# A two-layer attention and ConvFFN trunk on one core: the residual's split copy 288 bytes further on, two small reorderings beside it

## The chip, the core and the metric

One core of one Trainium2 chip runs the whole program in one launch. The metric is the device time of one execution in microseconds (us). Before the change three runs gave 598.50, 600.23 and 598.19 us: median 598.5 us.

## What is computed

A causal decoder trunk of two layers over 256 tokens of width 1024, in float32, with a final RMSNorm. Layer 0 mixes MoBA and differential attention, layer 1 dilated attention and a latent (MLA) attention; each layer ends in a gated ConvFFN with 2816 channels.

```python
def rmsnorm(x, g):
    y = xf * lax.rsqrt(jnp.mean(xf * xf, axis=-1, keepdims=True) + EPS)
    return y * g
...
h = h + even_mixer(rmsnorm(h, even_norm1[i]), ...)       # layer 0
h = h + odd_mixer(rmsnorm(h, odd_norm1[i]), ...)         # layer 1
h = h + conv_ffn(rmsnorm(h, ffn_norm[layer]), ...)       # after each mixer
...
return rmsnorm(h, final_norm)
# in odd_mixer, the latent part
q  = heads(rmsnorm(cq,  q_norm)  @ w_uq, ...)
kv = heads(rmsnorm(ckv, kv_norm) @ w_ukv, ...)
# in conv_ffn
u, g = jnp.split(h @ w_in, 2, axis=-1)
return (gelu(causal_conv(g)) * u) @ w_out
```

## The kernel before

**Splitting.** TensorE multiplies in the type fp32r. To keep float32 accuracy every operand is split into a rounded high part and a remainder, and a product a*b is made as three matmuls: high*high, low*high, high*low. Weights come in 100 pieces of up to 1 MB from HBM (`raw`, queue of SP), ScalarE makes the high part `whi` (line 152), VectorE the low part `wlo` (line 148). They are read once, so the program streams about 105 MB of weights and keeps TensorE busy beside it.

**The residual.** `hT` holds the residual, 1024 channels as 8 blocks `k` of 128 partitions, 256 tokens wide. `xs` (line 232) holds its split copy, scaled by the norm's gain: for each `k` 256 high values and behind them 256 low values, so one `k` is 2,048 bytes of a partition and `xs` is 16,384. `make_xhat` writes it (line 240 on ScalarE the high half, line 242 on VectorE the low half): once at the start and once in each of three `close_phase` calls. All input projections of both mixers and both FFNs read it.

**Who reads `xs`, and as which operand.** A TensorE matmul has a stationary operand (loaded first, the rows PEld LDWEIGHTS) and a moving one that streams past it.

- `passmajor` and `colmajor` (lines 296 to 311): weight stationary, 256 columns of `xs` moving, three matmuls for each `k` and weight block. The program has 1,152 such matmuls.
- `product` (line 903) in the FFN blocks f = 5 to 21 of each layer: for each `k` one matmul of the high weight with high and low halves together (512 columns of `xs`), and one of the low weight with the high half (256 columns). That is 17 x 2 x 8 = 272 pairs in a layer, 544 in all.
- `vjob` (line 313): `xs` is stationary here, 512 columns of weights move; 3 calls of `v_units` x 2 x 8 x 3 = 144 matmuls.

The other large group are the output projections: `proj_tile` (line 482), with weights stationary and 256 columns of an activation tile `o` moving, and in the last FFN `proj_tail` (line 850), with `o` stationary and 512 or 256 columns of weights moving. In layer 1 `uq_unit` and `ukv_unit` (lines 722 and 737) move 256 columns of the latent tiles `cqh`, `cql`, `ckr`.

**Where the tiles lie.** Pools are laid out one behind another in each partition. The built program places `hT` at byte 129,312 and `xs` at byte 137,504, which is 32 past a multiple of 64 and 288 past a multiple of 512. All `whi` and `wlo` buffers are also 288 past a multiple of 512. All tiles of pool `two` (`o`, `cqh`, `cql`, `ckr`, `qk` and others) are 64 past one. Pools `tmp`, `work` and `two` lie behind `xs`.

**Order.** TensorE's order is written by hand for the whole program. In the start and in the FFN main loop the other engines' order is by hand too; in the attention stages a scheduler orders ScalarE, VectorE and GpSimd. The norm's scale is not applied to `xs` but later: squares of the residual are summed by four small matmuls (`pss`), `rsqrt` (line 256) makes the scale, and its broadcast (`psb`) multiplies what the projections leave.

**The latent stage (`u0`, line 665).** After the projections `cq` and `ckv` are in the banks `pc` and `pk`, ScalarE and VectorE split them into `cqh`, `cql`, `ckr` (lines 675 and 676); then ScalarE squares both (678, 679) and GpSimd adds the two halves of the first square (680). `col_sums` in `u2` sums the squares by matmuls (`pss<-ones,sqc`).

**The last norm (lines 953 to 977).** For each of five tiles of the result `TAIL`, ScalarE squares with an accumulated sum (959), VectorE multiplies the tile by the gain into `y` (960). With the last tile of a row block VectorE makes the mean (966), GpSimd the power -0.5 (969), ScalarE and VectorE scale one half of `y` each (973, 975), and two DMAs write them.

Of the kernel before, what the change touches and what calls it, by code (L numbers as in the profile page):

```python
# [22 lines left out]
F32R = mybir.dt.float32r  # L23
AF = mybir.ActivationFunctionType
ALU = mybir.AluOpType
# [3 lines left out]
S = 256  # L29
D = 1024  # L30
KD = D // 128
# [72 lines left out]
def trunk(ctx, tc, x, rel_bias, small, lam_p, wpack, fin_g, onehot, addrow, tab, out):  # L104
    nc = tc.nc
# [3 lines left out]
    xpool = ctx.enter_context(tc.tile_pool(name="xpool", bufs=1))  # L109
# [10 lines left out]
    def t2(name, dt=F32, shape=(128, 2, S)):  # L120
        return two.tile(list(shape), dt, name=name, tag="t2")
# [4 lines left out]
    def pair(a):  # L126
        return a.rearrange("p (a b) -> p a b", a=2)
# [101 lines left out]
    subg = consts.tile([128, 1], F32)  # L229


    xs = xpool.tile([128, KD, 2, S], F32R, name="xs")
    xh, xl = xs[:, :, 0], xs[:, :, 1]
    sqs = {}

# [319 lines left out]
    def two_pairs(ca, cb):  # L555
        a, b = need(ca), need(cb)
        pa, pb = bank("pd"), bank("pd")
        colmajor([(pa[:, 0:S], True, a, 0), (pa[:, S:], False, a, 128),
                  (pb[:, 0:S], True, b, 0), (pb[:, S:], False, b, 128)])
        return pa, pb  # L560

    def stats1(env):
        env['r_col'] = norm_cols()
        env['r_diag'] = diags(env['r_col'], 2)
# [95 lines left out]
    def odd_layer():  # L660
# [4 lines left out]
        def u0():  # L665
            pc, pk = box['p'] = two_pairs('ocq', 'ock')
            stats1(env)
            cqh, cql = t2("cqh", F32R), t2("cql", F32R)
            ckr = t2("ckr", F32R)
            s1, s2 = t2("sqc"), t2("sqk", shape=(128, S))  # L670
            for i in range(3):
                src = pc[:, i * S:(i + 1) * S] if i < 2 else pk[:, 0:S]
                hi, lo = (cqh[:, i], cql[:, i]) if i < 2 else (ckr[:, 0], ckr[:, 1])
                g = gcol[:, QNORM + i:QNORM + i + 1]
                nc.scalar.activation(hi, src, AF.Copy, scale=g)
                nc.vector.scalar_tensor_tensor(lo, src, g, hi.bitcast(F32), op0=ALU.mult,
                                               op1=ALU.subtract)
            nc.scalar.activation(s1, pair(pc), AF.Square)
            nc.scalar.activation(s2, pk[:, 0:S], AF.Square)
            nc.gpsimd.tensor_tensor(s1[:, 0], s1[:, 0], s1[:, 1], op=ALU.add)  # L680
            kt = t2("krt")
            nc.vector.tensor_tensor(kt[:, 0], pk[:, S:], tab_t, op=ALU.mult)
            box.update(cqh=cqh, cql=cql, ckh=ckr[:, 0], ckl=ckr[:, 1], sq=[[s1[:, 0]], [s2]], kt=kt)
# [79 lines left out]
        def u6():  # L763
            ukv_unit(1)
            uq_unit(2)
            uq_unit(3)

        units = [(None, u0), (None, u1), (None, u2), kc0[0], (None, u3), (None, u5), (None, u6)]
        units += qk_units(env, 'oq1', ('q2', 'q3'), 'r_q') + qk_units(env, 'ok1', ('k2', 'k3'), 'r_bc')
        units += v_units(env, 'ovc', 'vc')  # L770
# [13 lines left out]
    def ffn(l, final):  # L784
# [65 lines left out]
        def proj_tail(f, i):  # L850
            w = weights(f)
            (oh, ol), (hi, lo) = acts[f], w
            tb, c0, c1 = TAIL[i]
            a = box['acc'][i][:, :c1 - c0]
            s = slice(tb * 128, (tb + 1) * 128)
            mm(a, oh[:, s], hi[:, f % 2, c0:c1], False, False)
            mm(a, ol[:, s], hi[:, f % 2, c0:c1], False, False)
            mm(a, oh[:, s], lo[:, f % 2, c0:c1], False, f == NF - 1)

        if final:  # L860
            fin_t = [t2("fin", shape=(128, 512)) for _ in range(2)]
# [88 lines left out]
        def piece(t, tb, c0, c1):  # L950
            return t[2 * tb + c0 // 512][:, c0 % 512:c0 % 512 + c1 - c0]

        for i, (tb, c0, c1) in enumerate(TAIL):
            for f in range(NF - LAGF, NF):
                proj_tail(f, i)
            h, o = box['acc'][i][:, :c1 - c0], piece(y, tb, c0, c1)
            q = i if tb == 0 else i - 2
            t = t2("fsq", shape=(128, c1 - c0))
            nc.scalar.activation(t, h, AF.Square, accum_out=ss[tb][:, q:q + 1])
            nc.vector.tensor_tensor(o, h, fin_t[c0 // 512][:, c0 % 512:c0 % 512 + c1 - c0], op=ALU.mult)  # L960
            if q == 0:
                nc.vector.tensor_scalar(ss[tb][:, 0:1], ss[tb][:, 0:1], EPS * D, None, op0=ALU.add)
            if tb == 1 and q == 1:
                nc.vector.tensor_add(ss[tb][:, 0:1], ss[tb][:, 0:1], ss[tb][:, 1:2])
            if c1 == D:
                nc.vector.tensor_scalar(ss[tb][:, q:q + 1], ss[tb][:, q:q + 1], ss[tb][:, 0:1], 1.0 / D,
                                        op0=ALU.add, op1=ALU.mult)
                r = ss[tb][:, 3:4]
                nc.gpsimd.tensor_tensor(r, ss[tb][:, q:q + 1], mhalf[:, 0:1], op=ALU.pow)
                for c in range(2):  # L970
                    o = y[2 * tb + c]
                    if c == 0:
                        nc.scalar.activation(o, o, AF.Copy, scale=r)
                    else:
                        nc.vector.tensor_scalar(o, o, r, None, op0=ALU.mult)
                    (nc.scalar if c == 0 else nc.sync).dma_start(
                        out[tb * 128:(tb + 1) * 128, c * 512:(c + 1) * 512], o)
# [32 lines left out]
    def late_loads():  # L1010
# [6 lines left out]
        return lam_t  # L1017
    even_layer()
    ffn(0, False)
    odd_layer()  # L1020
    ffn(1, True)


# [68 lines left out]
```

## Time and profile before

| | |
|---|---|
| runs before, us | 598.50, 600.23, 598.19 (median 598.5) |
| profiled execution, us | 597.86, of which the span from first to last instruction is 596.1 |
| granted TensorE clock, mean over the span | 0.998 of full speed (2.4 GHz) |
| TensorE matmul busy | 588.3 us, 99% of the span |
| VectorE, ScalarE, GpSimd busy | 74%, 58%, 12% |
| HBM read | 104.92 MB, 178 GB/s over the span |

The profiled execution lies 0.64 us, or 0.1%, under the median. Matmuls overlap in the records (one's duration reaches past the start of the next), so TensorE's pace is read from the starts of successive matmuls, not from durations: the start of a later row less the start of an earlier one, divided by the matmuls between them. A row `x2` stands for two matmuls.

### The profile page before, as it was taken

Reading aid. Unit: us, or ns where it says so; the run is one execution under the profiler, and the core shown is the slowest. Engines: PE = TensorE matmul, PEld = TensorE weight load, DVE = VectorE, ACT = ScalarE, POOL = GpSimd, SP = SyncE. Lnnn points to the kernel's source line nnn. Section 1 sums busy time; section 2 is a strip of 40 time slices with the busy share of each in tenths; the row PEclk is TensorE's granted clock in tenths of the full one; section 3 lists DMA queues with packets and bytes.
Section 4 is the critical chain, followed back from the end, with each engine's and each line's share of the span. In section 5 each row is a group of like instructions: output and inputs, shape, how many; then the busy total and the mean of one; then the engine's idle time right before and its main releaser. Section 6 shows DMA issues by size and latency. Waiting matters only on the chain.

```text
span 596.1 us, 10372 instructions
## 1 busy us (share of the span) xinstructions
PE 588.3 (99%) x4078; PEld 542.7 (91%) x4078; DVE 441.1 (74%) x789; ACT 348.3 (58%) x643; POOL 69.7 (12%) x81
## 2 busy tenths in 40 slices
PE   9999999999999999999999999999999999999996
PEld 9989989999999999999999998999988888888885
DVE  5795966779777777877696975558967778777752
ACT  6757656548566555665554755646665556655532
POOL 1000001032011011101034000005110111001110
PEclk9999999999999999999999999999999999999999
DMA  8966645425544655455425343344535554554301
GB/s 293 383 230 222 222 142 191 164 82 205 211 163 189 213 212 192 165 208 194 165 103 221 134 145 137 142 172 147 213 142 211 212 196 167 203 196 167 132 1 71
DMA packets 20265, 106.67 MB, mean 179 GB/s; under 512 B 2478, under 2 KB 6008, under 8 KB 8568
## 3 DMA queue, kind: packets, MB, share of 16 engines
q1 hardware_dynamic: 16424, 101.68, 46.7%
q10 hardware_dynamic: 3632, 3.80, 2.1%
q8 instruction: 32, 0.52, 0.3%
q0 software_dynamic: 160, 0.52, 0.3%
q14 instruction: 17, 0.14, 0.1%
HBM read 104.92 MB, written 1.08 MB: 178 GB/s over the span
## 4 chain that ended last, share of the span: by engine, by line
PE 94%; issue 2%; POOL 2%; ACT 1%; DVE 1%; POOLq 0%; ACTq 0%
PE pd L124 52%; PE acc L124 26%; PE pv L124 6%; PE pS L124 2%; PE pO L124 2%; PE puq L124 1%; PE warm L124 1%; POOL sqt L251 1%; PE pukv L124 1%; PE pT L374 0%; PE pT L375 0%; PE pT L376 0%; PE psb L124 0%; PE pss L124 0%; POOL sqc L680 0%
## 5 line engine op out<-in xcount | busy, mean ns | idle before, releaser
L124 PE MATMUL pd<-xs,whi 128*128 128x256 f32 (+1 forms) x1312 | 326.3, 330 | 0.0
L124 PE MATMUL pd<-xs,wlo 128*128 128x256 f32 x928 | 252.2, 281 | 0.0
L148 DVE TENSOR_TENSOR wlo<-raw,whi 128x1024 fp32r<-128x1024 f32 (+1 forms) x191 | 233.8, 1249 | 20.3 <-ACT whi L152 20.2
L124 PEld LDWEIGHTS pd<-xs,whi 128*128 128x128 f32 x1312 | 218.2, 190 | 22.9 <-ACT sqt L247 0.6
L152 ACT ACTIVATE whi<-raw 128x1024 fp32r<-128x1024 f32 (+1 forms) x191 | 193.6, 1040 | 59.2 <-PE pd L124 20.5
L124 PEld LDWEIGHTS pd<-xs,wlo 128*128 128x128 f32 x928 | 172.4, 190 | 0.0
L124 PE MATMUL acc<-o,whi 128*128 128x256 f32 x608 | 108.7, 281 | 0.0
L124 PEld LDWEIGHTS acc<-o,whi 128*128 128x128 f32 x608 | 92.7, 188 | 1.0 <-issue 0.2
L124 PE MATMUL acc<-o,wlo 128*128 128x256 f32 x304 | 84.7, 279 | 0.0
L911 ACT ACTIVATE lowp<-pd 128x256 f32<-128x256 f32 x68 | 25.8, 379 | 79.8 <-PE pd L124 79.8
L807 POOL TENSOR_TENSOR ge<-ge,gbuf 128x256 f32<-128x256 f32 x44 | 37.1, 845 | 291.1 <-ACT ge L806 291.1
L912 DVE TENSOR_TENSOR ug<-pd,lowp 128x256 f32<-128x256 f32 x68 | 28.5, 420 | 50.3 <-ACT lowp L911 50.3
L124 PE MATMUL acc<-whi,o 128*128 128x512 f32 (+1 forms) x220 | 58.2, 350 | 0.2 <-ACT o L812 0.2
L124 PEld LDWEIGHTS acc<-o,wlo 128*128 128x128 f32 x304 | 57.1, 188 | 0.0
L124 PEld LDWEIGHTS acc<-whi,o 128*128 128x128 f32 x220 | 38.3, 188 | 7.5 <-ACT o L812 0.7
L124 PE MATMUL acc<-wlo,o 128*128 128x512 f32 (+1 forms) x110 | 38.6, 351 | 0.0
L813 DVE TENSOR_TENSOR o<-ge,o 128x256 fp32r<-128x256 f32 x44 | 19.0, 438 | 21.5 <-ACT o L812 21.5
L363 ACT ACTIVATE ex<-sc,nm 128x256 f32<-128x256 f32 (+1 forms) x56 | 24.8, 444 | 15.4 <-DVE nm L360 12.0
L794 ACT ACTIVATE t<-gbuf,ccol 128x256 f32<-128x256 f32 x44 | 26.4, 601 | 12.0 <-DVE gbuf L935 10.1
L812 ACT ACTIVATE o<-ge 128x256 fp32r<-128x256 f32 x44 | 18.4, 418 | 23.1 <-POOL ge L807 23.1
L124 PE MATMUL pv<-whi,xs 128*128 128x512 f32 x96 | 30.1, 395 | 0.0
L242 DVE SCALAR_TENSOR_TENSOR xs<-hT,gcol,xs 128x256 fp32r<-128x256 f32 x32 | 24.3, 803 | 5.3 <-ACT xs L240 5.3
(153 smaller groups left out, 501.2 us busy)
## 6 DMA issues: line engine op xcount, KB each, us to landing
raw<-in_wpack_dram SPq DMA_DIRECT2D x91, 1024.0 KB, 4.8
raw<-in_wpack_dram SPq DMA_DIRECT2D x5, 512.0 KB, 6.0
Tt<-btab ACTq DMA_DIRECT2D x3, 512.0 KB, 5.8
raw<-in_wpack_dram SPq DMA_DIRECT2D x4, 256.0 KB, 5.0
raw_t<-in_wpack_dram SPq DMA_DIRECT2D x4, 256.0 KB, 5.7
Tt<-btab ACTq DMA_DIRECT2D x1, 1024.0 KB, 6.3
hT<-in_x_dram ACTq DMA_DIRECT2D x4, 128.0 KB, 4.1
hT<-in_x_dram SPq DMA_DIRECT2D x2, 256.0 KB, 5.5
```

Of the source, the lines that this page charges most:

```text
L124: nc.tensor.matmul(o, l, r, start=start, stop=stop, skip_group_check=True)
L148: nc.vector.tensor_tensor(lo[:, s], raw, hi[:, s].bitcast(F32), op=ALU.subtract)
L152: nc.scalar.activation(splits[i][:, s], raw, AF.Copy)
L242: nc.vector.scalar_tensor_tensor(xl[:, k], hT[:, k], gcol[:, g0 + k:g0 + k + 1], xh[:, k].bitcast(F32), op0=ALU.mult, op1=ALU.subtract)
L251: eng.tensor_tensor(sqs['a'], sqs['a'], t, op=ALU.add)
L363: nc.scalar.activation(e[:, a:b], t[:, a:b], AF.Exp, bias=nm[:, i:i + 1], scale=-1.0, accum_out=den[:, i:i + 1])
L794: nc.scalar.activation(t1, g[:, 2:], AF.Identity, bias=col(f, 3), scale=col(f, 2))
L807: nc.gpsimd.tensor_tensor(ge, ge, gbuf[f % 3][:, 0, 2:], op=ALU.mult)
L812: nc.scalar.activation(o[:, 0], ge, AF.Copy)
L813: nc.vector.tensor_tensor(o[:, 1], ge, o[:, 0].bitcast(F32), op=ALU.subtract)
L911: nc.scalar.activation(lowp, p[:, S:], AF.Copy)
L912: nc.vector.tensor_tensor(t[:, i], p[:, :S], lowp, op=ALU.add)
```

## The change

Three edits.

1. The tile for `xs` is made 128 elements (512 bytes) longer, and `xs` starts 72 elements (288 bytes) into it. In the built program the residual's copy then starts at byte 137,792, which is a multiple of 64 and 64 past a multiple of 512, as the tiles of pool `two` are. The pools behind it move by 512 bytes, so their places within 512 bytes are what they were; `hT`, `whi` and `wlo` stay where they were.
2. In `u0` the three instructions on squares stand ahead of the split.
3. In the last norm, for a row block's last tile, the product with the gain stands behind the mean.

```diff
-    xs = xpool.tile([128, KD, 2, S], F32R, name="xs")
+    xbuf = xpool.tile([128, KD * 2 * S + 128], F32R, name="xs")
+    xs = xbuf[:, 72:72 + KD * 2 * S].rearrange("p (k a s) -> p k a s", k=KD, a=2)
     xh, xl = xs[:, :, 0], xs[:, :, 1]
...
             s1, s2 = t2("sqc"), t2("sqk", shape=(128, S))
+            nc.scalar.activation(s1, pair(pc), AF.Square)
+            nc.gpsimd.tensor_tensor(s1[:, 0], s1[:, 0], s1[:, 1], op=ALU.add)
+            nc.scalar.activation(s2, pk[:, 0:S], AF.Square)
             for i in range(3):
...
-            nc.scalar.activation(s1, pair(pc), AF.Square)
-            nc.scalar.activation(s2, pk[:, 0:S], AF.Square)
-            nc.gpsimd.tensor_tensor(s1[:, 0], s1[:, 0], s1[:, 1], op=ALU.add)
             kt = t2("krt")
...
-            nc.vector.tensor_tensor(o, h, fin_t[c0 // 512][:, c0 % 512:c0 % 512 + c1 - c0], op=ALU.mult)
+            if c1 < D:
+                nc.vector.tensor_tensor(o, h, fin_t[c0 // 512][:, c0 % 512:c0 % 512 + c1 - c0], op=ALU.mult)
...
             if c1 == D:
                 nc.vector.tensor_scalar(ss[tb][:, q:q + 1], ss[tb][:, q:q + 1], ss[tb][:, 0:1], 1.0 / D,
                                         op0=ALU.add, op1=ALU.mult)
+                nc.vector.tensor_tensor(o, h, fin_t[c0 // 512][:, c0 % 512:c0 % 512 + c1 - c0], op=ALU.mult)
                 r = ss[tb][:, 3:4]
```

No engine gains or loses an instruction, and TensorE's order is the same to the last matmul. Two pieces move.

ScalarE in `u0`, before (`sqc` and `sqk` are the squares, `cqh` and `ckr` the high parts of the split, `whi` weight pieces):

```order
L152 ACTIVATE whi<-raw 128x1024 x3
L675 ACTIVATE cqh<-pd,gcol 128x256
L152 ACTIVATE whi<-raw 128x1024 x2
L675 ACTIVATE cqh<-pd,gcol 128x256
L675 ACTIVATE ckr<-pd,gcol 128x256
L678 ACTIVATE sqc<-pd 128x512
L679 ACTIVATE sqk<-pd 128x256
L152 ACTIVATE whi<-raw 128x1024 x4
```

and now:

```order
L152 ACTIVATE whi<-raw 128x1024 x3
L672 ACTIVATE sqc<-pd 128x512
L674 ACTIVATE sqk<-pd 128x256
L679 ACTIVATE cqh<-pd,gcol 128x256
L152 ACTIVATE whi<-raw 128x1024
L679 ACTIVATE ckr<-pd,gcol 128x256
L679 ACTIVATE cqh<-pd,gcol 128x256
L152 ACTIVATE whi<-raw 128x1024 x5
```

Both squares have moved ahead of three split instructions and two weight pieces, and one weight piece has moved behind the split.

VectorE at the end of the program, the second row block, before (`fss` holds the sums of squares, `y` the result):

```order
L960 TENSOR_TENSOR y<-acc,fin 128x256
L964 TENSOR_TENSOR fss_6522<-fss_6522 128x1
L960 TENSOR_TENSOR y<-acc,fin 128x256
L966 TENSOR_SCALAR fss_6522<-fss_6522 128x1
L975 TENSOR_SCALAR y<-y,fss_6522 128x512
```

and now:

```order
L962 TENSOR_TENSOR y<-acc,fin 128x256
L966 TENSOR_TENSOR fss_6522<-fss_6522 128x1
L968 TENSOR_SCALAR fss_6522<-fss_6522 128x1
L970 TENSOR_TENSOR y<-acc,fin 128x256
L978 TENSOR_SCALAR y<-y,fss_6522 128x512
```

The mean (966, now 968) has moved ahead of one product with the gain. In the first row block the same two instructions have changed places.

## Rows read from the trace of the kernel before

**Rows 1.** The page, part 1: engine, busy us, share of the span, instructions

```profile
PE 588.3 (99%) x4078; PEld 542.7 (91%) x4078; DVE 441.1 (74%) x789; ACT 348.3 (58%) x643; POOL 69.7 (12%) x81
```

**Rows 2.** Waits, TensorE: who waited for whom, us in total, times, longest

```profile
PE pss L124 <- POOL sqc L680: 0.6, 1, 0.6
PE acc L124 <- ACT o L812: 0.2, 1, 0.2
```

**Rows 3.** Timeline, TensorE, layer 1 input projections: start us, us, engine, line, operation

```profile
303.92 0.40 PE L124 MATMUL pd<-xs,whi 128*128 128x256 f32 x2
...
314.00 0.40 PE L124 MATMUL pd<-xs,whi 128*128 128x256 f32 x2
```

**Rows 4.** Timeline, TensorE, output projection of layer 1's mixer, end

```profile
388.02 0.40 PE L124 MATMUL acc<-o,whi 128*128 128x256 f32 x2
...
401.67 0.40 PE L124 MATMUL pd<-xs,whi 128*128 128x256 f32 x2
```

**Rows 5.** Timeline, TensorE, end of layer 0's FFN, 120 matmuls of its output projection

```profile
288.71 0.40 PE L124 MATMUL acc<-o,whi 128*128 128x256 f32 x2
...
302.85 0.40 PE L124 MATMUL pd<-xs,whi 128*128 128x256 f32 x2
```

**Rows 6.** Timeline, TensorE, latent projections of layer 1

```profile
330.11 0.28 PE L124 MATMUL puq<-cqh,whi 128*128 128x256 f32 x1
...
331.16 0.40 PE L124 MATMUL pukv<-ckr,whi 128*128 128x256 f32 x2
```

**Rows 7.** Timeline, TensorE, products of FFN blocks 5 and 7 of layer 0

```profile
148.99 0.40 PE L124 MATMUL pd<-xs,whi 128*128 128x512 f32 x1
...
154.64 0.41 PE L124 MATMUL acc<-o,whi 128*128 128x256 f32 x2
...
165.84 0.39 PE L124 MATMUL pd<-xs,whi 128*128 128x512 f32 x1
...
171.39 0.40 PE L124 MATMUL acc<-o,whi 128*128 128x256 f32 x2
```

**Rows 8.** Timeline, TensorE, weights moving: vjob of layer 0, then proj_tail of layer 1

```profile
85.05 0.62 PE L124 MATMUL pv<-whi,xs 128*128 128x512 f32 x2
...
89.82 0.40 PE L124 MATMUL acc<-o,whi 128*128 128x256 f32 x2
...
441.41 0.62 PE L124 MATMUL acc<-whi,o 128*128 128x512 f32 x2
...
443.50 0.40 PE L124 MATMUL acc<-whi,o 128*128 128x256 f32 x2
```

**Rows 9.** Groups by shape, TensorE: xcount, then busy us and mean ns of one

```profile
L124 PE MATMUL pd<-xs,wlo 128*128 128x256 f32 x928 | 252.2, 281 | 0.0
L124 PE MATMUL pd<-xs,whi 128*128 128x512 f32 x544 | 190.5, 392 | 0.0
L124 PE MATMUL pd<-xs,whi 128*128 128x256 f32 x768 | 135.9, 287 | 0.0
```

**Rows 10.** Timeline, ScalarE and GpSimd, stage u0 of layer 1

```profile
314.73 0.46 ACT L675 ACTIVATE cqh<-pd,gcol 128x256 fp32r<-128x256 f32 x1
...
319.18 0.60 ACT L678 ACTIVATE sqc<-pd 128x512 f32<-128x512 f32 x1 [0.69 <-DVE cql L676]
...
315.13 1.63 POOL L259 TENSOR_TENSOR r_col<-rs,mhalf 128x2 f32<-128x2 f32 x1 [5.59 <-DVE rs L258]
319.85 1.80 POOL L680 TENSOR_TENSOR sqc<-sqc 128x256 f32<-128x256 f32 x1 [3.09 <-ACT sqc L678]
```

**Rows 11.** Timeline, all engines, the end of the program

```profile
590.75 0.42 DVE L960 TENSOR_TENSOR y<-acc,fin 128x256 f32<-128x256 f32 x1 [0.92 <-ACT fsq L959]
591.09 0.21 DVE L966 TENSOR_SCALAR fss<-fss 128x1 f32<-128x1 f32 x1
591.37 0.56 POOL L969 TENSOR_TENSOR fss<-fss,mhalf 128x1 f32<-128x1 f32 x1 [4.61 <-DVE fss L966]
```

**Rows 12.** Windows: stretch, its length, then busy us (and instructions) of PE, PEld, DVE, ACT, POOL

```profile
401.00:436.00 35.00, 35.00 (x286) 34.55 (x285) 31.51 (x44) 23.69 (x38) 11.53 (x11) 1.00 0.50 183
```

## The prediction

> **What bounds the kernel now.** I read the share of each engine first, then who waited for whom, then the starts of matmuls in the timeline. TensorE is busy 588.3 of the 596.1 us of the span [rows 1], and its waits for other engines are tenths of a us: 0.6 us once for the latent squares, 0.2 us once for an activation [rows 2]. So the kernel is a single stream of some four thousand matmuls, and its time is the pace of that stream. A wait can give back less than 1 us; a change of pace counts for every matmul. What is to be seen next is that the pace is not the same everywhere, although the engine is granted its full 2.4 GHz, where 256 columns take 106.7 ns.
>
> - With 256 columns of `xs` moving, 84 matmuls stand between starts 303.92 and 314.00 [rows 3]: 10.08 us / 84 = 120.0 ns each, 13.3 ns over the columns.
> - With 256 columns of `o` moving past the same kind of weights, 117 matmuls stand between 388.02 and 401.67 [rows 4]: 13.65 / 117 = 116.7 ns, 10.0 ns over the columns. At the end of layer 0's FFN it is 14.14 us for 120 [rows 5]: 117.8 ns.
> - With the latent tiles moving, 9 matmuls stand between 330.11 and 331.16 [rows 6]: 116.7 ns.
>
> The operations, the type, the weights' buffers and the run of three matmuls into one place are the same. What sets `xs` apart is where it lies: 32 bytes past a multiple of 64, while `o`, `cqh`, `cql` and `ckr` lie on one. The latent rows matter because they are made like an input projection and still go at the faster pace.
>
> **Edit 1, the place of `xs`, is the large term.** After it `xs` starts on a multiple of 64, and indeed at the same place within 512 bytes as `o`, against weights that stay where they are. So where `xs` moves, the nearest row is that of `o`.
>
> *256-column matmuls.* All matmuls into `pd` that move 256 columns are 928 + 768 [rows 9]; 544 of the 928 belong to products, which leaves 1,152. The gain of one lies between 0 (the place doesn't matter) and 120.0 - 116.7 = 3.3 ns; by rows 5 it is 2.2 ns. The sum is 2.5 to 3.8 us by the two paces; I take 3.2 us. Not all of it stays: between layer 1's norm and the first output projection TensorE already waits 0.2 us for an activation [rows 2], and VectorE is busy 31.51 of 35 us there [rows 12]. The norm's chain does not get shorter, so of the 0.8 us that the 240 matmuls there could gain I let 0.5 us turn into more of that wait, and keep 2.7 us.
>
> *Products.* FFN block 7 has 16 pairs between 165.84 and 171.39 [rows 7]: 5.55 / 16 = 346.9 ns for 768 columns, which take 320.0; so 13.4 ns over for each of two matmuls, the same excess as the 256-column ones with `xs` have. No row of this kernel has 512 columns of an aligned tile moving past weights. Bounds: nothing, or the pace of rows 4 for both (10.0 ns over, 340.0 a pair, 6.9 less), and by rows 5 (11.2 over) 342.4, 4.5 less. For 544 pairs [rows 9] that is 0, 2.5 or 3.8 us; I take 5.7 ns, so 3.1 us, because the equal excess says that one cause is at work in both shapes. As a cover for a faster FFN, VectorE has the rest of its time: it is busy 74% over the span [rows 1], and a block that is 1.5% shorter asks for 1% more of it.
>
> *`vjob`.* Here `xs` is stationary and weights move: 21 matmuls between 85.05 and 89.82 [rows 8], 227.1 ns each. In the last FFN weights move too, but past `o`, an aligned stationary: 9 matmuls between 441.41 and 443.50 [rows 8], 232.2 ns. After the change `xs` is aligned as `o` is, so I take the slower pace: 144 x 5.1 ns = 0.7 us lost. Bounds: 0 and 1 us.
>
> What is written to `xs`, and the pools behind it (moved by 512 bytes), I cost at nothing: VectorE and ScalarE are not waited for where that happens beyond what stands above, and the pools keep their place within 512 bytes.
>
> **Edit 2, the squares.** The sum on GpSimd ran from 319.85 for 1.80 us [rows 10], because ScalarE squared only at 319.18 after waiting for VectorE, and TensorE waited for its end: 0.6 us of idle matmul time [rows 2], 0.7 with the weight load that starts afresh. ScalarE was at the first part of the split at 314.73 [rows 10]; now the square stands there and ends at about 315.4. GpSimd is in its power until 315.13 + 1.63 = 316.76 [rows 10] and can end the sum by 318.6 even at its slow 1.80 us, some 2.5 us ahead of need. The wait goes wholly: -0.7 us. The split of the latents moves back by the two squares (some 1 us), and a weight piece behind it by about as much. `cqh` is first read at 330 [rows 6], so the cover is more than 10 us; without it 1 us would be lost. What is late next is nothing: the matmuls behind `pss` have their operands.
>
> **Edit 3, the last scale.** The end of the program is a chain of waits: product with the gain 590.75, mean 591.09, power 591.37, scaling, DMA [rows 11]. The mean takes the product's place and starts 591.09 - 590.75 = 0.34 us earlier; the product then runs under the power (0.42 against 0.56 us) and is done before the scaling on VectorE. -0.3 us, between 0.1 and 0.4.
>
> **The sum.** -2.7 - 3.1 + 0.7 - 0.7 - 0.3 = -6.1 us against the profiled execution's 597.86, which gives 591.8. That execution lies 0.64 us under the median of the three runs; I forecast 592.0 us.
>
> **A rule that speaks against edit 1.** The rows give 120.0 and 116.7 ns for the same shape in two places [rows 3, 4]. The Trainium skill (TensorE: Matmul & The Clock Gate, Step-by-step: what each phase is for) gives TensorE two independent read ports, so that loading weights takes nothing from the running matmul, and (SBUF — State Buffer, Specifications) lines of 16 bytes, on which `xs` started before as it does now. By these pages edit 1 changes no pace, and the time would be that of the first rival. Rows 3, 4 and 6 disagree: neither rule accounts for the 3.3 ns.
>
> **The rivals.**
>
> 1. *The place of `xs` changes nothing.* The difference between 120.0 and 116.7 ns would come from the order in which banks are filled, or from what ran ahead. For it: `acc` and `pd` use banks in another way, and `o` itself goes at 116.7 and 117.8 [rows 4, 5]. Against it: the latent rows, built like `pd`, go at 116.7 [rows 6]. Only edits 2 and 3 count: 597.86 - 1.0 = 596.9 us.
> 2. *Products keep their pace.* The pair may be held by the load of the second weight under a long matmul, not by the moving operand. Then -2.7 + 0.7 - 1.0 = -3.0: 594.9 us. Against it stands only the equal excess of 13.4 ns.
> 3. *Products fall into their slow pace, and the others keep theirs.* Block 5 of the same FFN took 148.99 to 154.64 for the same 16 pairs [rows 7]: 353.1 ns a pair, 6.2 more than block 7. The same matmuls can settle at another pace, then, and operands placed differently settle slower in rows 8. If all pairs went so: 544 x 6.2 ns = +3.4 us, with +0.7 for `vjob` and -1.0 that is +3.1: 601.0 us. It decides only if the 256-column matmuls gain less than about 1 us; with their 2.7 the two cancel and the time is within 1 us of before. Against it: past weights placed as here, an aligned moving tile is never slower than `xs` in any row.
>
> **How the numbers follow.** A measurement of this kernel can tell about 0.3%, 1.8 us, from no change. The forecast (both shapes gain, at paces between rows 4 and 5 or a little beyond) has 0.66, with its own range 589.0 to 594; rival 2 has 0.15; rival 1 has 0.12; rival 3 has 0.07. Forecast and rival 2 are faster by more than 1.8 us; rival 1 lies on the edge (1.6 us under the median), of which I count a third as faster. Faster 0.85, same 0.08, slower 0.07. The range goes from 588.8 (3.8 + 3.8 + 0.7 + 0.3 gained, nothing lost, and 0.5 more if the 528 output matmuls of layer 0's FFN go from the pace of rows 5 to that of rows 4) to 597.4, which takes in rivals 1 and 2 with the spread of the runs, and leaves out rival 3 and the edges of the forecast.
>
> **What would show it.** In the profile after: the same stretch of `pd<-xs` with 256 columns starts every 117 to 118 ns, not 120.0 (edit 1 right); products stand at 340 to 343 ns a pair, not 347; `pv` goes at about 232 ns. TensorE has no wait for `sqc`, and its square runs at 315. The power at the end starts 0.2 us after the mean with the product beside it. If the pair stands at 347, rival 2 holds; if `pd` stands at 120.0, rival 1; a pair at 353 is rival 3. The forecast is wrong as a whole if the pace does not follow the place of the moving tile.

## The result and the profile after

| | before | after |
|---|---|---|
| median of 6 runs each, us (lowest to highest) | 598.50 (597.77 to 600.23) | 594.62 (594.06 to 595.54) |
| profiled execution, us; its span | 597.86; 596.1 | 594.06; 592.3 |
| granted TensorE clock over the span | 0.998 | 1.0 |
| TensorE matmul busy, us | 588.3 | 584.7 |

The ratio is 0.9934, with a 95% interval of 0.9922 to 0.9945: 3.9 us faster. The forecast was 592.0 us, 2.6 us lower, with the range 588.8 to 597.4. The clock does not explain the gain: of the six executions after, one had a granted clock of 0.997 and took 594.09 us, another 1.0 and took 594.06. One execution further down stands apart and is left out of its kernel's median and ratio: of ten of the kernel with triples at 32 bytes one took 3304.54 us, the other nine 595.95 to 598.37.

TensorE is still the whole bound. The page's part 1 of the changed kernel (engine, busy us, share, instructions) answers to [rows 1]:

```profile
PE 584.7 (99%) x4078; PEld 538.9 (91%) x4078; DVE 441.5 (75%) x789; ACT 347.8 (59%) x643; POOL 69.7 (12%) x81
```

Its waits (who for whom, us in total, times, longest) answer to [rows 2]. The wait for `sqc` is gone and the one for `o` is as long as it was; the wait for `xs` is at the program's start, before the first projection. Both kernels also wait once for 1.0 us at the very start, in the matmuls of `warm`.

```profile
PE pd L124 <- ACT xs L241: 0.5, 1, 0.5
PE acc L124 <- ACT o L813: 0.2, 1, 0.2
```

The timeline of TensorE (start us, us, engine, line, operation), end of layer 0's FFN and the first projections of layer 1, for [rows 5] and [rows 3]:

```profile
287.31 0.40 PE L124 MATMUL acc<-o,whi 128*128 128x256 f32 x2
...
301.31 0.40 PE L124 MATMUL pd<-xs,whi 128*128 128x256 f32 x2
...
312.51 0.50 PE L124 MATMUL pss<-ones,sqt 128*128 128x1 f32 x4
```

From 301.31 to 312.51 stand 96 matmuls with 256 columns of `xs`: 11.20 / 96 = 116.7 ns, where it was 120.0. The 120 of `o` ahead of them take 14.00 us, 116.7 ns each, where they took 117.8, although nothing about `o` was changed.

The same view at FFN block 5 and at `vjob` of layer 0, for [rows 7] and [rows 8]:

```profile
148.22 0.39 PE L124 MATMUL pd<-xs,whi 128*128 128x512 f32 x1
...
153.77 0.40 PE L124 MATMUL acc<-o,whi 128*128 128x256 f32 x2
```

```profile
84.75 0.40 PE L124 MATMUL pv<-wlo,xs 128*128 128x512 f32 x1
...
89.89 0.28 PE L124 MATMUL acc<-o,whi 128*128 128x256 f32 x1
```

Sixteen pairs in 5.55 us are 346.9 ns a pair. Block 5 was at 353.1 and has come down to this; block 7 was here already, and stayed. `vjob` has 22 matmuls in 5.14 us: 233.6 ns, where it was 227.1.

Stage `u0` on four engines, for [rows 10], and the program's end, for [rows 11]:

```profile
312.91 0.58 ACT L672 ACTIVATE sqc<-pd 128x512 f32<-128x512 f32 x1
...
313.29 1.63 POOL L260 TENSOR_TENSOR r_col<-rs,mhalf 128x2 f32<-128x2 f32 x1 [5.25 <-DVE rs L259]
314.89 0.74 POOL L673 TENSOR_TENSOR sqc<-sqc 128x256 f32<-128x256 f32 x1
314.95 0.97 DVE L275 TENSOR_TENSOR diag<-ident,r_col 128x256 f32<-128x256 f32 x1 [0.60 <-POOL r_col L260]
...
315.65 0.28 PE L124 MATMUL pd<-xs,wlo 128*128 128x256 f32 x1
316.07 0.67 PE L124 MATMUL psb<-diag,ones 128*128 128x256 f32 x2
```

```profile
587.23 0.21 DVE L968 TENSOR_SCALAR fss<-fss 128x1 f32<-128x1 f32 x1 [0.92 <-ACT fsq L960]
587.36 0.41 DVE L970 TENSOR_TENSOR y<-acc,fin 128x256 f32<-128x256 f32 x1
587.52 0.55 POOL L972 TENSOR_TENSOR fss<-fss,mhalf 128x1 f32<-128x1 f32 x1 [4.86 <-DVE fss L968]
```

GpSimd adds the squares right behind its power, at 314.89 in place of 319.85, and takes 0.74 us in place of 1.80. But VectorE's `diag`, which starts 0.06 us behind it, takes 0.97 us here and 0.42 in the other three places of the program (and here before), and TensorE's `psb` waits for it: from 315.65 to 316.07 is 0.30 us more than one matmul's pace. At the end the product runs beside the power. In the kernel before, VectorE started a weight piece together with GpSimd's sum of [rows 10]:

```profile
319.85 1.22 DVE L148 TENSOR_TENSOR wlo<-raw,whi 128x1024 fp32r<-128x1024 f32 x1
```

The tally, from the starts of all 4,078 matmuls of the two traces, grouped by shape and operand:

| what | forecast, us | measured, us | how |
|---|---|---|---|
| 256 columns of `xs`, 1,152 | -2.7 | -3.4 | 119.8 to 116.8 ns each |
| products, 544 pairs | -3.1 | -0.3 | 347.4 to 346.8 ns a pair |
| `vjob`, 144 | +0.7 | +0.8 | 227.7 to 233.4 ns |
| squares | -0.7 | -0.5 | the wait gone, a shorter one for `diag` come |
| last scale | -0.3 | -0.3 | from the last matmul's start to the span's end: 6.15 to 5.88 us |
| 256 columns of `o`, 912 | 0 | -0.7 | 117.4 to 116.7 ns |
| `proj_tail`, 330 | 0 | -0.1 | |
| waits and starts elsewhere, most of them before 63 us | 0 | +0.7 | the rest |
| span | -6.1 | -3.8 | 596.1 to 592.3 |

The time up to 63 us, where most of the last row but one lies, differs by 0.2 to 0.3 us either way between this profile and those of two kernels below that have the same paces there (`xs` at 32 bytes, the sum on VectorE). The one large term that failed is products.

### The profile page after: what moved, and what is told of

Its sections match the earlier page's. It is cut to its first block, busy times and chain, and to the rows that moved or that the text cites. A ratio compares the mean times of both kernels' runs of the same rounds, so it can differ in the third digit from the quotient of the medians.

```text
span 592.3 us, 10372 instructions
## 1 busy us (share of the span) xinstructions
PE 584.7 (99%) x4078; PEld 538.9 (91%) x4078; DVE 441.5 (75%) x789; ACT 347.8 (59%) x643; POOL 69.7 (12%) x81
## 4 chain that ended last, share of the span: by engine, by line
PE 95%; DMA 1%; ACT 1%; issue 1%; DVE 0%; POOL 0%; POOLq 0%; ACTq 0%
PE pd L124 54%; PE acc L124 27%; PE pv L124 6%; PE pS L124 2%; PE pO L124 2%; DMA hT<-in_x_dram 1%; PE puq L124 1%; PE psb L124 1%; PE pukv L124 1%; PE pT L375 0%; PE pT L376 0%; PE pT L377 0%; PE pss L124 0%; PE acc L842 0%; ACT whi L152 0%
## 5 line engine op out<-in xcount | busy, mean ns | idle before, releaser
L124 PE MATMUL pd<-xs,whi 128*128 128x256 f32 (+1 forms) x1312 | 322.5, 327 | 0.6 <-ACT xs L241 0.5
L124 PEld LDWEIGHTS pd<-xs,whi 128*128 128x128 f32 x1312 | 215.7, 188 | 22.5 <-ACT xs L241 0.7
```

What stands on the lines that cost most here:

```text
L124: nc.tensor.matmul(o, l, r, start=start, stop=stop, skip_group_check=True)
```

## Experiments

Medians are in us. Where nothing else is said, an edit is made to the changed kernel. Each run's kernel of before, on the same chip, stood at 598.2 to 598.3, and its ratio is against that.

**The parts by themselves.** The first run has edit 1 alone, the second edits 2 and 3 alone.

```diff
# first run: edits 2 and 3 undone, xbuf as in the change
# second run
-    xbuf = xpool.tile([128, KD * 2 * S + 128], F32R, name="xs")
-    xs = xbuf[:, 72:72 + KD * 2 * S].rearrange("p (k a s) -> p k a s", k=KD, a=2)
+    xs = xpool.tile([128, KD, 2, S], F32R, name="xs")
```

> Edit 1 alone: the residual's copy 288 bytes further, squares and last mean in the old order. If the three edits add up, this run lacks 0.7 us (TensorE's wait for the latent squares is back) and 0.3 us (the last chain) of what the whole change gave: some 2.9 us under before, near 595.6. Input projections with 256 columns of xs at 116.7 ns a matmul, products near 346.8 ns a pair, vjob near 233 ns, as in the changed kernel. Rival: edit 1 gives all or nearly all of the gain, because the wait for the squares had been cover for something else; then it is within 0.3 us of the changed kernel.

> Edits 2 and 3 alone, the residual's copy at its old place. If they add up: 1.0 us under before, no wait of TensorE for the squares, matmuls at their old paces (120.0 ns for 256 columns of xs, 346.9 a pair, vjob 227). Rival: the moved squares delay the latents' split and the time is as before.

Edit 1 alone: 595.58, ratio 0.9953 (0.9939 to 0.9967). Edits 2 and 3 alone: 597.62, ratio 0.9992 (0.9984 to 1.0001). The gains, 2.6 and 0.5 us, add up to 3.1, near the 3.9 of the whole; in the profiled spans 3.1 and 0.6 add up to 3.7, of 3.8. By its medians the second run cannot be told from no change. With edit 1 alone the wait for `sqc` is back, and GpSimd's sum takes 1.81 us again:

```profile
PE pss L124 <- POOL sqc L681: 0.7, 1, 0.7
```

With edits 2 and 3 alone every pace is that of before (119.8 ns, 347.4 a pair, `vjob` 227.7, `o` 117.4), so the paces, `o`'s too, come from the place of `xs`. Matched matmul by matmul, the starts between 311 and 331 us gain 0.55 us there and nothing after. Why it is not the 0.7 of the forecast, or more, the next run asks.

**The sum on VectorE.** GpSimd's sum now overlaps `diag`. Here VectorE makes it, behind `diag`.

```diff
-            nc.gpsimd.tensor_tensor(s1[:, 0], s1[:, 0], s1[:, 1], op=ALU.add)
+            nc.vector.tensor_tensor(s1[:, 0], s1[:, 0], s1[:, 1], op=ALU.add)
```

> The changed kernel with the sum of the latent squares on VectorE, behind diag, in place of GpSimd. Theory (GpSimd's sum at 314.9 holds up VectorE's diag, 0.97 us where it takes 0.42 elsewhere, and TensorE's psb waits for diag: 0.30 us from the last projection matmul to psb beyond one matmul's pace): diag is back at 0.42 us, psb follows without that gap, 0.3 us gained between 311 and 331 us, 594.3 us. Rival (diag is long because of where xs or sqc lies, or of the power on GpSimd ahead of it): diag stays at 0.97 us and the gap at 0.3 us; 594.6 us.

594.23, ratio 0.9933 (0.9917 to 0.9950). The timeline of VectorE and TensorE at the same place:

```profile
315.18 0.42 DVE L275 TENSOR_TENSOR diag<-ident,r_col 128x256 f32<-128x256 f32 x1 [0.60 <-POOL r_col L260]
...
315.88 0.28 PE L124 MATMUL pd<-xs,wlo 128*128 128x256 f32 x1
...
316.00 0.59 PE L124 MATMUL psb<-diag,ones 128*128 128x256 f32 x2
```

`diag` is at 0.42 again and `psb` follows 0.12 us behind the last matmul, at the stream's pace. Matched matmul by matmul against the changed kernel, this stage gains 0.37 us and no other from 45 us on gains or loses more than 0.03. So edit 2 gave back 0.4 of the 0.9 us that it took away, by a collision of its own. In the medians 0.4 us cannot be told from no change.

**Other places of `xs`.** Was it the start on a multiple of 64 that counted?

```diff
-    xs = xbuf[:, 72:72 + KD * 2 * S].rearrange("p (k a s) -> p k a s", k=KD, a=2)
+    xs = xbuf[:, 8:8 + KD * 2 * S].rearrange("p (k a s) -> p k a s", k=KD, a=2)     # first run, 32 bytes
+    xs = xbuf[:, 16:16 + KD * 2 * S].rearrange("p (k a s) -> p k a s", k=KD, a=2)   # second run, 64 bytes
```

> All three edits, but the copy moved by 32 bytes, not 288: it starts on a multiple of 64, at another place within 512 bytes than the activation tiles. Theory A (the start of the moving operand within 64 bytes decides): 116.7 ns for 256 columns of xs, and the time of the changed kernel, 594 to 595. Theory B (it must stand at the place of the activation tiles within 512 bytes): 120.0 ns, some 597.

> All three edits, but the copy moved by 64 bytes: it starts 32 bytes past a multiple of 64, as before, and no longer at the place of the weight buffers within 512 bytes. Theory A (start within 64 bytes): 120.0 ns for 256 columns of xs, vjob 227 ns, time 597 to 598. Theory C (it was slow because moving and stationary operands stood at the same place within 512 bytes): below 118 ns, and the time of the changed kernel.

At 32 bytes: 594.54, ratio 0.9935 (0.992 to 0.995), all paces as at 288. At 64 bytes: 598.25, ratio 1.0000 (0.9991 to 1.0008). There `xs` starts 32 past a multiple of 64, as in the kernel before, yet 256 columns do not go at 120.0 ns. TensorE's timeline, the first projections of layer 1 and those after its mixer:

```profile
304.27 0.40 PE L124 MATMUL pd<-xs,whi 128*128 128x256 f32 x2
...
315.58 0.50 PE L124 MATMUL pss<-ones,sqt 128*128 128x1 f32 x4
...
402.35 0.39 PE L124 MATMUL pd<-xs,whi 128*128 128x256 f32 x2
...
413.24 0.50 PE L124 MATMUL pss<-ones,sqt 128*128 128x1 f32 x4
```

Both stretches have 96 matmuls: 117.8 ns and 113.4 ns, with one code and one place. Products slow down to 352.2 ns a pair and `vjob` to 233.4; together these take back what 256 columns gain. What edits 2 and 3 gain is lost at the start, where the first bias matmul (`psbt`) comes at 19.00 us for 18.03 before. So the alignment is not the cause, and one place can have several paces.

**The pace at many places.** The next kernel leaves the trunk out: nothing but the three shapes, 136 matmuls at each of 25 placements of `xs` and of the weights, in two buffers of its own. It was executed once, at a granted clock of 1.0. In the diff the last line stands for the loops.

```diff
+    for dx, dw in COMBOS:                    # bytes from the buffers' starts
+        hi, lo, xs = views(dx, dw)
+        # 48 matmuls of 256 columns into pd, 32 pairs into pu and pg, 24 as vjob into pv
```

> The pace by itself: this program leaves the whole trunk out and runs only matmuls, on data without meaning. For 25 pairs of places (xs so many bytes past a multiple of 512, weights so many) it runs in turn 48 matmuls of the input projections' form (256 columns of xs past weights), 32 pairs of the products' form (512 then 256 columns) twice over, and 24 of vjob's form (512 columns of weights past xs). Theory C (only the distance between the two operands within some power of two counts): the pace at distance 0 is 120.0, 346.9 and 227 ns, at 32 and 288 it is 116.7, 346.8 and 233, at 64 116.9, 352 and 233, wherever the weights lie, and the pairs at weights 32 or 64 repeat those at weights 0. Theory A (the start of the moving operand within 64 bytes) has fallen for the input projections and would show 120.0 at 16, 32, 48 and 96 alike. Theory D (the pace depends on what the stream did before, not on the place): the same distance gives different paces in its repetitions. If some distance gives products below 343 ns, a better place than that of the change exists; if none, the products' pace is not to be had by moving xs.

TensorE's timeline at distance 0 (`xs` less weights, in bytes), at 32, at 32 again with the weights moved by 32 too (`xs` 64), and at 192. A row x48 has the 256-column matmuls; from the first x16 to x24 are 32 pairs:

```profile
36.07 5.92 PE L79 MATMUL pd<-xs,whi 128*128 128x256 f32 x48
41.82 3.00 PE L79 MATMUL pu<-xs,whi 128*128 128x512 f32 x16
...
53.13 5.61 PE L79 MATMUL pv<-whi,xs 128*128 128x512 f32 x24
...
80.82 5.76 PE L79 MATMUL pd<-xs,whi 128*128 128x256 f32 x48
86.42 2.95 PE L79 MATMUL pu<-xs,whi 128*128 128x512 f32 x16
...
97.53 5.76 PE L79 MATMUL pv<-whi,xs 128*128 128x512 f32 x24
...
215.60 5.62 PE L79 MATMUL pd<-xs,whi 128*128 128x256 f32 x48
221.05 2.98 PE L79 MATMUL pu<-xs,whi 128*128 128x512 f32 x16
...
232.35 5.66 PE L79 MATMUL pv<-whi,xs 128*128 128x512 f32 x24
...
462.78 5.76 PE L79 MATMUL pd<-xs,whi 128*128 128x256 f32 x48
468.38 2.95 PE L79 MATMUL pu<-xs,whi 128*128 128x512 f32 x16
...
479.49 5.76 PE L79 MATMUL pv<-whi,xs 128*128 128x512 f32 x24
```

Distance 0: 5.75 us for 48 and 11.31 us for 32 pairs. Distance 32: 5.60 and 11.11, and the same to the hundredth of a us with both moved. Distance 192: 5.45 for the 48, but 11.30 for the pairs. Settled, the first matmuls at each place and the whole of the program's first place, which begins slower, left out, in ns (the distance is that of `xs` from the weights in all three rows, also in `vjob`, where the weights move):

| distance, bytes | 0 | 16 | 32 | 48 | 64 | 96 | 128 | 160 | 192 | 224 |
|---|---|---|---|---|---|---|---|---|---|---|
| 256 columns | 120.0 | 118.6 | 116.7 | 118.3 | 117.8 | 120.0 | 118.6 | 118.8 | 113.3 | 118.4 |
| pair | 353.3 | 346.5 | 346.7 | 349.9 | 353.3 | 350.0 | 350.9 | 346.6 | 353.3 | 353.2 |
| `vjob` | 226.7 | 226.7 | 233.4 | 233.4 | 233.2 | 234.5 | 231.9 | 233.2 | 228.9 | 233.3 |

At 256, 288, 352 and 384 bytes stand the values of 0, 32, 96 and 128 again; with the weights moved, those of the distance that is left. At 320 and 448, and at 64 and 192 with other weights, one of the three values differs (348.9 for 353.3, or 117.8 for 113.3). So the pace follows the distance between the two operands, modulo 256 bytes, with more than one value at some distances. What in the chip makes it so, no run here shows. Blocks of `xs` lie 1,024 bytes apart and blocks of weights 512, so all matmuls of a stream have one distance. The kernel before is at distance 0 (both 288 past a multiple of 512), the changed one at 32, and `o` is and was at 32. No pair goes under 346.5 ns at any place tried.

**Which pace, and what ran before.** The second probe, also without the trunk, takes 20 distances and comes to each in four ways: from another place, from itself, from `vjob`, from pairs. Its 256-column blocks are triples (high weight with high and with low half, low weight with high half), put into a bank as a product would put them. It too was executed once, at a granted clock of 1.0.

> Again the trunk is left out. For 20 distances of xs from the weights this runs three matmuls of 256 columns per k (high weight with high and with low half, low weight with high half) into the banks of a product: what a product would cost without its 512-column matmul. Each distance is entered four times, after itself, after vjob's form and after the products' form. If the distance alone decides, the four agree, 120.0 ns at 0, 116.7 at 32, and the 113.3 ns that the first probe showed at 192 comes each time: a product would then cost 3 x 113.3 = 340 ns, less than the 346.7 that no place of xs went under. If what ran before decides too, 192 gives 113.3 after one entry and 117.8 after another, and can't be counted on.

TensorE's timeline at distance 112, then at the first and at the second of two visits to 192 (blocks of 24 matmuls; `pv` is `vjob`, `pd` four pairs):

```profile
201.03 2.88 PE L78 MATMUL pb<-xs,whi 128*128 128x256 f32 x24
203.75 1.59 PE L78 MATMUL pv<-whi,xs 128*128 128x512 f32 x6
...
351.37 2.88 PE L78 MATMUL pa<-xs,whi 128*128 128x256 f32 x24
354.09 2.88 PE L78 MATMUL pb<-xs,whi 128*128 128x256 f32 x24
...
504.52 2.99 PE L78 MATMUL pa<-xs,whi 128*128 128x256 f32 x24
507.35 2.99 PE L78 MATMUL pb<-xs,whi 128*128 128x256 f32 x24
...
514.32 2.88 PE L78 MATMUL pg<-xs,whi 128*128 128x256 f32 x24
517.04 1.57 PE L78 MATMUL pd<-xs,whi 128*128 128x512 f32 x8
```

At the second visit to 192, which comes from 240, it is 2.83 / 24 = 117.9 ns when the block follows itself and 2.72 / 24 = 113.3 after `vjob`. At the first visit, which comes from 184, the block that follows itself takes 2.72 / 24 = 113.3 as well. So a block that follows itself keeps the pace it had, within 0.3 ns at all places but the program's first; the distance sets a few possible paces and what ran before picks one. At 32 there are two as well: 117.7 entered from 24 and then from itself, 116.7 after `vjob` and after pairs. At 112 all four ways end at 113.3, which no other place does.

**`o` moved too.** Pool `two` 160 bytes further, so `o` is at distance 192.

```diff
-    xbuf = xpool.tile([128, KD * 2 * S + 128], F32R, name="xs")
+    xbuf = xpool.tile([128, KD * 2 * S + 168], F32R, name="xs")
```

> The changed kernel with pool two (the activation tiles o, the latent tiles) another 160 bytes on, so that o stands 192 bytes from the weights within 256 and xs stays at 32. If the first probe's 113.3 ns at 192 holds for o: 912 output matmuls and 60 latent ones gain 3.4 ns each, 3.3 us, and the time is near 591.3. If they settle at the probe's other pace for that distance, 117.8: 1.0 us slower than the changed kernel, near 595.6. If places within 256 bytes don't matter for o: 594.6.

593.17, ratio 0.9916 (0.9899 to 0.9932). TensorE's timeline, end of layer 0's FFN and output projection of layer 1's mixer:

```profile
287.02 0.40 PE L124 MATMUL acc<-o,whi 128*128 128x256 f32 x2
...
301.15 0.28 PE L124 MATMUL pd<-xs,whi 128*128 128x256 f32 x1
...
385.07 0.28 PE L124 MATMUL acc<-o,wlo 128*128 128x256 f32 x1
...
398.44 0.40 PE L124 MATMUL pd<-xs,whi 128*128 128x256 f32 x2
```

The first has 120 matmuls, 117.8 ns; the second 118, 113.3 ns. Both paces of the second probe are here in one kernel.

**Products as triples, `xs` at 112 bytes, and both.** Four kernels: both; 112 with pairs kept; triples at the change's place; both with `o` at 192.

```diff
-    xs = xbuf[:, 72:72 + KD * 2 * S].rearrange("p (k a s) -> p k a s", k=KD, a=2)
+    xs = xbuf[:, 28:28 + KD * 2 * S].rearrange("p (k a s) -> p k a s", k=KD, a=2)
...
-                mm(p, hi[:, 8 * i + k], xs[:, k], k == 0, False)
+                mm(p[:, :S], hi[:, 8 * i + k], xs[:, k, 0], k == 0, False)
+                mm(p[:, S:], hi[:, 8 * i + k], xs[:, k, 1], False, False)
                 mm(p[:, :S], lo[:, 8 * i + k], xs[:, k, 0], False, k == KD - 1)
```

> Edits as in the changed kernel, but xs lies 112 bytes past its buffer's start (so 112 past the weights modulo 256), and a product's 512-column matmul is written as two of 256. Theory (the distance of moving from stationary operand, modulo 256 bytes, sets the possible paces): in the probe the distance of 112 gave 113.3 ns for 256 columns whatever ran before. So col256 117 -> 113.3 ns (1,152 of them: -3.9 us), a product's step 346.8 -> 340.0 ns (544 of them: -3.7 us) against the changed kernel's 594.6: 587.0 us. Rival (the probe's pace does not carry over to a kernel whose other engines use the SBUF too, a matmul more costs what it costs in the probe at 32 bytes): col256 stays at 117 or more, a step is 350 or more: 596.3 us or more.

> As the run before, but products stay pairs of 512 and 256 columns. Theory: col256 at 113.3 ns, -3.9 us; the pair at 112 bytes was not measured, its neighbours at 96 and 128 bytes gave 350 to 351 ns and no place under 346.5, so 0 to +3.5 us: 590.7 to 594.3 us, taken 592.4. Rival (113.3 belongs to the probe): col256 at 117 or more, 594.6 us or more.

> The changed kernel with products as triples of 256 columns, xs where the change put it. Theory: at this distance a 256-column matmul takes 116.7 ns, so a step is 350.0 ns in place of 346.8: +1.7 us, 596.3 us. Rival (a pair is held by the load of the second weight under a long matmul, which shorter matmuls take away): a step under 346.8, the time under 594.6 us.

> The first of these four with o moved too, to 192 bytes past the weights. Theory: 1.4 us under the first (as moving o alone gave 593.2 against 594.6): 585.6 us, o at 113.3 in part of the kernel and 117.8 elsewhere. Rival (o's pace depends on what ran before, and another pace of the products ahead sends it to 117.8 everywhere): the same as the first or up to 1 us slower.

| | median | ratio (95%) | 256 columns of `xs` | a product's step | `o` |
|---|---|---|---|---|---|
| both | 592.42 | 0.9896 (0.9879 to 0.9913) | 114.5 | 344.2 | 116.7 |
| 112, pairs | 595.64 | 0.9952 (0.9938 to 0.9966) | 114.5 | 352.9 | 116.8 |
| triples at 32 | 596.90 | 0.9978 (0.9966 to 0.9990) | 116.8 | 350.0 | 116.7 |
| both, `o` at 192 | 588.30 | 0.9824 (0.9809 to 0.9840) | 114.4 | 344.3 | 114.0 |

With pairs, 112 bytes lose on products (+3.3 us) what 256 columns gain (-2.7): the sixteen pairs of block 7 [rows 7], in TensorE's timeline of that kernel, take 5.65 us, 353.1 ns each. The expectation had no value for a pair there, and its 350 to 351 of the neighbours was too low.

```profile
164.08 0.39 PE L124 MATMUL pd<-xs,whi 128*128 128x512 f32 x1
...
169.73 0.28 PE L124 MATMUL acc<-o,whi 128*128 128x256 f32 x1
```

Triples at the change's place cost what was expected: 350 a step for 346.8. Splitting the long matmul frees nothing by itself. Triples at 112 gain, but 2.2 us where 7.6 were expected. In the profiled spans it is 1.8: the stretches of 256 columns give 2.3 of the 3.9 expected and products 1.4 of 3.7, while the start loses 1.5 and `proj_tail` 0.4. One reason is in TensorE's timeline of an FFN block of layer 1 in the kernel with both:

```profile
497.65 0.39 PE L124 MATMUL pd<-xs,whi 128*128 128x256 f32 x2
...
499.43 0.39 PE L124 MATMUL pd<-xs,whi 128*128 128x256 f32 x2
...
503.17 0.40 PE L124 MATMUL acc<-whi,o 128*128 128x512 f32 x1
```

The first 15 matmuls take 118.7 ns each, the next 33 take 113.3. So it is in every block of layer 1, and some 10 matmuls in every block of layer 0: this stream needs that long behind `o` to find its pace, and loses it at each change. Streams of `o` at 32 stand at 116.7 from their first matmuls, so this is not so of every stream. The expectation took the probe's settled pace alone; there too the first 24 matmuls at 112 after `vjob` had taken 116.7 ns each. The other reason is its start: the first bias matmul is 1.6 us later (19.55 for 17.94), since pieces of weights come later, as its waits show. All three kernels with triples have this, but triples are not needed for it: the kernel at 64 bytes, with as many instructions as the change, has 1.1 us of it (19.00), and the one with pairs at 112 has 0.2 (18.13). Why the load is later is open, and so is the loss in `proj_tail`.

```profile
PE pd L124 <- ACT whi L152: 1.5, 2, 0.9
```

The last kernel, with `o` at 192, is the fastest of all: 588.3 us, 10 us under before. The 585.6 that was expected rested on 587.0 for the kernel with both, which had not come. Its timeline at the end of layer 0's FFN:

```profile
285.50 0.40 PE L124 MATMUL acc<-o,whi 128*128 128x256 f32 x2
...
299.10 0.42 PE L124 MATMUL pd<-xs,whi 128*128 128x256 f32 x2
```

These 120 matmuls of `o` take 113.3 ns; at the same place, behind pairs at distance 32, they took 117.8. Moving `o` was worth 1.4 us there and is worth 4.1 us here (1.2 and 3.8 in the profiled spans), and the rival, which had the products ahead send `o` to its slow pace, is refuted: they send it to the fast one.

## Why the prediction was right, and where it was not

The time came out inside the whole range, but not by the way that was forecast: 594.62 lies outside the 589.0 to 594 that the forecast gave itself, and the range held it by taking in rival 2.

1. **256 columns of `xs`: right in size, wrong in reason.** The forecast of 116.7 to 117.8 came out as 116.7. But the reason given, the start on a multiple of 64, fell with the run at 64 bytes. What held was the other half of that sentence: `xs` was put at the same place within 512 bytes as `o`, and so at `o`'s distance from the weights. That the nearest row had the right distance was luck: the prediction did not look for a distance. The 0.5 us set aside for a wait behind VectorE was not needed; that wait is 0.2 us as before.
2. **Products: the step that failed** is "because the equal excess says that one cause is at work in both shapes". 13.4 and 13.3 ns over were equal by chance of the distance 0. At 32 the 256 columns stand at 10.0 over and the pair at 2 x 13.3; at 192 at 6.6 and 2 x 16.7. The term was -3.1 and measured -0.3, a miss of 2.8 us, which is more than the whole error of 2.3 us in the span. Rival 2 held, the chance of 0.15, with its 594.9 us against 594.62. That it came so close is in part luck too: in the span it had -3.0 against -3.8, and 0.7 more from 256 columns of `xs` and 0.7 from `o`, which it did not have, stand against 0.7 of waits and starts. Its reason, the load of the second weight under a long matmul, is not shown: three shorter matmuls with a load more go at 350 a step at the place of the change, slower than the pair, and at 340 where they settle at 112. Why a pair never went under 346.5 ns stays open.
3. **Block 5's slow pace** [rows 7], left as a curiosity and a rival, was the clue: at distance 0 a pair has two paces, 346.9 and 353.1 in the kernel before, and the probe shows the slower, 353.3. At 32 every block of layer 0 stands at 346.7 and every block of layer 1 at 346.9.
4. **`vjob`** lost 0.8 us for 0.7, as forecast from the row of `o` as stationary, which had the right distance.
5. **Squares: the step "What is late next is nothing" failed** by a small sum. The wait for `sqc` went as described, but the sum, now right behind GpSimd's power, starts with `diag`, which waits for the same power, and holds it up: -0.5 us where -0.7 was forecast and where the run with the sum on VectorE comes to -0.9. In the kernel before the sum itself was the one held up: it started together with a `wlo` of VectorE at 319.85, which took 1.22 us, and took 1.80 us [rows 10] for the 0.74 of after. The Trainium skill (SBUF — State Buffer, Who interferes with whom) has VectorE with two inputs and GpSimd share a port pair, as a lock that the first to start holds. Both cases agree with that: the one held up ends 0.6 us (the sum, before) and 0.3 us (`diag`, after) behind the end of the other. So does the run with the sum on VectorE, where `diag` takes 0.42 us.
6. **Last scale**: -0.3 us, as worked out.
7. **Missed**: `o` in layer 0's FFN went from 117.8 to 116.7 (-0.7 us) without being moved. The forecast had this in the lower end of its range alone. The second probe has both paces at `o`'s distance of 32, 117.7 and 116.7, by what ran ahead; here that is the products, at another place.

The Trainium skill's rule that spoke against edit 1 (TensorE: Matmul & The Clock Gate, Step-by-step: what each phase is for) was that two read ports make loading free for the running matmul. The first probe has 256 columns from 113.3 to 120.0 ns with the clock granted in full and the places alone changed, and the measurement decides; whether it is the loading that takes the difference is not shown. The Trainium skill (TensorE: Matmul & The Clock Gate, Back-to-back issue gap) gives an isolated matmul its columns plus 2.5 ns as the gap to the next. The streams here have a weight load for each matmul, and the lowest settled excess of 256 columns in them is 6.6 ns.

## What to carry to other kernels

When a kernel is one stream of matmuls, read its pace for each shape and stage from the starts, and compare same shapes with different operands: a difference of 3% is worth looking for in where operands lie. Try a few distances between moving and stationary operand (here it repeated every 256 bytes) in the kernel itself, every shape that uses the tile at once, since a place that is best for one can be worst for another, and since a neighbouring stream can pick the pace of the next. Where an instruction is moved ahead on GpSimd, look at what VectorE then runs beside it. Two shapes with the same excess need not have the same cause: price each by a row of its own, and where there is none, keep "no change" as a likely case.

## What the runs showed of the hardware

- The pace of a stream of matmuls with a weight load each depends on the distance between moving and stationary operand, modulo 256 bytes: 113.3 to some 120 ns for 256 columns, 346.5 to 353.3 for a pair of 512 and 256, 226.7 to 234.5 for 512 columns past a 128-column stationary of `xs`.
- One distance can have two paces or more (113.3, 117.8 at 192; 346.9, 353.1 for pairs at 0). What ran ahead picks one, and in the second probe it stayed when a block followed itself.
- A sum on GpSimd lengthened VectorE's product `diag` from 0.42 to 0.97 us when it started 0.06 us ahead of it.
- A stream can need some matmuls to settle after a change: 10 to 15 for `xs` at 112 behind `o` in the kernel with both, while `o` at 32 had its pace at once.
